# Wide value and key products in the second half of a streaming encoder step, and its queries in a new place

## The chip, the cores and the metric

One core of a Trainium2 chip. The metric is the device time of one execution of the whole kernel in microseconds, as the median of several runs, without what the host does.

## The reference

One layer of a hybrid encoder. A prompt of 2048 frames and a sample of 64 frames, both 1024 wide, go through RMSNorm and one projection to 6144 columns:

```python
h = rmsnorm(x, norm_g) @ w_in
qa, ka, va, za, qb, kb, vb, zb, ga, gb = jnp.split(h, _split_points(), axis=-1)
```

The first four parts, 512 columns each, feed differential attention with four heads: queries and keys in two halves of 64, normalised, values of 128, a linear distance term, a chunked causal mask, and the difference of two softmaxes. The next four feed retention with four heads: a recurrence over chunks of 64 frames with a state of 128 by 128 per head. `za` and `zb` gate the two branches, `ga` and `gb` (1024 columns each) merge them:

```python
m = ga * (oa @ w_oa) + gb * (ob @ w_ob)
return x + m @ w_out
```

The sample attends to 4096 cached frames as well. Normalised keys, values and the retention states are outputs too.

## The kernel before, in words

All large products take float32 operands split in two parts, high and low, of a rounded type; a product is the sum of three on TensorE: high by high, high by low, low by high. So each weight that is loaded is cast (the high part, ScalarE, line 546) and subtracted (the low part, GpSimd, line 556, or VectorE for three of the first pieces, line 553).

The prompt is projected in two halves of 1024 frames (the sample goes with the first). There are two kinds of projection. `transposed` keeps weights in the array and streams 512 frames past them; it makes retention's queries and keys and all gates. `natural` keeps a tile of 128 frames in the array and streams the columns of weights: 256 at a time ("narrow"), two tiles of frames in one bank of PSUM, or 512 at a time ("wide"), one tile in a bank. Both go through `mm_group` (line 592), eight row blocks of the input by three products each. `fin_qk`, `fin_va` and `fin_vb` normalise, split and store what comes out; keys and queries are transposed on TensorE on the way.

Attention's values, keys and queries (`va`, `ka`, `qa`) are wide in the first half and narrow in the second, in two groups of 256 columns each, that is two heads: value, key and query of heads 0 and 1, a mark `kqv0`, then those of heads 2 and 3, a mark `kqv1`. Retention's values (`vb`) follow, wide in both halves, then retention's queries and keys, a mark `ret`, and the gates. `w_stream` writes this list; `w_load` and `w_split` follow it for the weights, one piece after the other.

The projected parts go to DRAM and come back: `h_loader` loads the keys and values of a head, `q_loader` its queries, and `head_in` lets them start some time after the head's mark. `z_stream` runs attention head by head, then the sample's attention (first half), and retention; TensorE takes its products in between those of the projections. Buffers are counted by tags: four each of `K` and `V` in the attention pool, sixteen of `w` for split weights, three of `ws` for weights as loaded. Where the split weights of a wide group lie is set by its number in the list (`w_room`): groups 0 and 2 (the first half's values and queries) take the `K` and `V` buffers, the others the `w` buffers.

After the projections, `out_stream` multiplies the gated branches by their output weights (`m_tile`), then by `w_out`: `y_quad` does 256 frames at a time with seven products (`SEVEN`) in place of eight, from sums of blocks that are made ahead. `out_prep` splits the output weights and gates the rows; it starts when attention and retention are done.

What sets the order: the kernel is written by a planner in Python. Each stage is a generator; `loop` takes the first by priority whose condition or time has come, and it issues instructions until it yields. The planner holds a clock for TensorE (`self.pe`) and estimates for the other engines; a buffer taken from `take` and an operand carry the time at which they are thought to be ready. So the order on each engine is fixed before the kernel runs, by estimates, and a change to one stage moves the instructions of all that follow. All loads and stores go through the queue of SyncE.

Of the kernel before, what the change touches and what calls it, by code (L numbers as in the profile page):

```python
# [71 lines left out]
class Hybrid:  # L72
# [464 lines left out]
    def w_piece(self, wait):  # L537
# [10 lines left out]
        return self.w_low(wide, n, st, h, l, th, tag, tags)  # L548

    def w_low(self, wide, n, st, h, l, t, tag, tags):  # L550
        th = t
        if n in (5, 7, 8):
            self.nc.vector.tensor_sub(l, st, h.bitcast(F32))
            t = self.V(512, t)
        else:
            self.nc.gpsimd.tensor_sub(l, st, h.bitcast(F32))  # L556
            t = self.G(512, t)
# [157 lines left out]
    def spawn_fin(self, fin, ps, r, n, nu, t0):  # L715
        t = self.pe + LAT
        done = fin(ps[:r, :n], r, nu, t0, t) if r == 128 else self.halves(ps[:, :n], n, t, fin, t0)
        self.spawn(done, 0, "w")
# [293 lines left out]
    def q_loader(self, half):  # L1012
        for h in range(4):
            yield from self.head_in(half, h)
# [3 lines left out]
    def head_in(self, half, h):  # L1018
        k = f"kqv{h // 2}{half}"
        yield lambda: k in self.done  # L1020
        yield self.marks[k] + 9000

    def h_loader(self, half):
        for h in range(4):
            yield from self.head_in(half, h)
            yield from self.load_head(half, h)
# [898 lines left out]
    def y_quad(self, g):  # L1925
# [3 lines left out]
        for k, (bank, b, need, done) in enumerate(SEVEN):  # L1929
# [14 lines left out]
            split = (g, k) == (7, 6)  # L1944
            for ct in range(4):
# [6 lines left out]
                if split:  # L1952
                    continue
# [7 lines left out]
            if split:  # L1961
                yield lambda: "x12" in q
                for u in range(2):
                    cols = slice(256 * u, 256 * u + 256)
                    for ct in range(4):
                        csl = slice(128 * ct, 128 * ct + 128)
                        for a, w in ((h, wh), (h, wl), (l, wh)):
                            nc.tensor.matmul(ps[:, cols], a[:, csl], w[:, ct, cols], start=False,
                                             stop=w is wh and a is l and ct == 3, skip_group_check=True)
                            t = self.P(256)  # L1970
                    self.y_last(q, ps, t, cols)
                    yield self.pe
                return
# [67 lines left out]

    def y_last(self, q, ps, t, cols):
        x = self.xr[q["g"]][0]["12"]
        self.nc.vector.tensor_add(x[:, cols], ps[:, cols], x[:, cols])
        self.V(256, max(t, q["x12"]))
        t0 = 256 * q["g"]
        self.st(self.o["y_prompt"][0, t0:t0 + 128, 512 + cols.start:512 + cols.stop], x[:, cols], 1 << 17)
# [93 lines left out]
    def w_stream(self):  # L2141
# [12 lines left out]
        first = ([wva, wk, wq, m0, m1], ORD(fva0, fva, fk, fq, m0, m1))  # L2154
# [11 lines left out]
        seqs = [f + seq for f in first]  # L2166
# [6 lines left out]
        self.npiece = 0  # L2173
        self.opened = False
# [22 lines left out]
    def mark(self, name):  # L2197
        yield lambda: True
        self.done.add(name)
        self.marks[name] = self.pe  # L2200

    def z_stream(self):
        for half in range(2):
            yield lambda: f"kqv0{half}" in self.done
# [143 lines left out]
```

## Time and profile before

| what | value |
|---|---|
| median of 3 runs | 1929.06 us (1927.94 to 1929.13) |
| the profiled execution: its time | 1928.88 us |
| its span | 1927.1 us |
| granted TensorE clock | 1.0 |
| TensorE, VectorE, ScalarE, GpSimd busy | 1919.5, 1134.2, 1005.1, 461.5 us |
| moved by DMA | 308.50 MB, 160 GB/s on average |

Names: PE is TensorE, PEld its weight loads, DVE VectorE, ACT ScalarE, POOL GpSimd, SP SyncE. `L592` is line 592 of the kernel. `mm<-wh,xh` is a product into the tile `mm` with the columns of `wh` streamed past the held tile `xh`. In a row of a group, "x384 | 110.8, 289" is the count, the busy time in us and the mean of one in ns. In a row of waits stand the total in us, the times, and the longest. The busy time of a product has a modelled end, and neighbours overlap. The sample's attention lies at about 500 to 670 us of the span, the first half's retention at about 740 to 830; the second half's narrow products begin at about 740 us, the output stage at 1570, the last group of products at 1920.

### The profile page before, as it was taken

How to read it: one execution, taken by the hardware profiler on the slowest of the kernel's cores; microseconds unless marked ns; L12 is line 12 of the kernel's file. 1: busy time of each engine (PE TensorE's matmuls, PEld its weight loads, DVE VectorE, ACT ScalarE, POOL GpSimd, SP SyncE). 2: the span in 40 equal slices, each digit the busy share in tenths (PEclk: the TensorE clock that was granted, in tenths of full speed). 3: DMA queues.
4: the chain of work that ended last, by engine and by line, in shares of the span. 5: the costliest groups of instructions: out<-in, count | busy, mean ns of one | idle time of the engine just before them, and what ended most of it. 6: DMA issues, size and time to landing. Idle time of an engine off the chain costs nothing.

```text
span 1927.1 us, 32956 instructions
## 1 busy us (share of the span) xinstructions
PE 1919.5 (100%) x11638; PEld 1709.5 (89%) x11638; DVE 1134.2 (59%) x2794; ACT 1005.1 (52%) x2137; POOL 461.5 (24%) x365
## 2 busy tenths in 40 slices
PE   9999999999999999999999999999999999999999
PEld 7878899999989999999988888888889889999887
DVE  6553576635565344646856656746664339987664
ACT  6442676655445544545756756645664535554221
POOL 2320121212121223212102211121221526522442
PEclk9999999999999999999999999999999999999999
DMA  7647563436656887664334243363233758886542
GB/s 250 211 144 185 140 184 118 122 84 166 169 159 172 226 225 210 177 193 145 102 106 140 86 129 101 105 189 107 73 112 101 236 172 247 257 252 205 173 153 77
DMA packets 356343, 308.50 MB, mean 160 GB/s; under 512 B 65745, under 2 KB 313809, under 8 KB 356178
## 3 DMA queue, kind: packets, MB, share of 16 engines
q1 hardware_dynamic: 356178, 306.39, 54.4%
q8 instruction: 92, 1.51, 0.4%
q14 instruction: 73, 0.60, 0.1%
HBM read 201.38 MB, written 99.88 MB: 156 GB/s over the span
## 4 chain that ended last, share of the span: by engine, by line
PE 95%; DVE 2%; DMA 2%; ACT 0%; issue 0%; SPq 0%; DVEq 0%; ACTq 0%
PE mm L592 55%; PE s L1071 3%; PE s L1072 3%; PE at L1179 3%; PE pv L1159 2%; PE pv L1158 2%; PE pv L1157 2%; PE s L1954 1%; PE s L1956 1%; PE s L1955 1%; PE pv L1425 1%; PE pv L1538 1%; PE at L1528 1%; PE tp L794 1%; PE mm L1954 1%; PE mm L1956 1%
## 5 line engine op out<-in xcount | busy, mean ns | idle before, releaser
L592 PE MATMUL mm<-xh,wh 128*128 128x512 f32 (+2 forms) x1280 | 457.5, 357 | 0.0
L592 PE MATMUL mm<-xh,wl 128*128 128x512 f32 (+2 forms) x1280 | 452.4, 353 | 0.0
L592 PE MATMUL mm<-xl,wh 128*128 128x512 f32 (+2 forms) x1280 | 451.9, 353 | 0.0
L556 POOL TENSOR_TENSOR wl<-ws,wh 128x512 fp32r<-128x512 f32 x189 | 255.2, 1364 | 655.4 <-ACT wh L546 480.2
L592 PEld LDWEIGHTS mm<-xh,wl 128*128 128x128 f32 x1280 | 240.9, 188 | 31.2
L592 PEld LDWEIGHTS mm<-xh,wh 128*128 128x128 f32 x1280 | 241.3, 189 | 29.1
L592 PEld LDWEIGHTS mm<-xl,wh 128*128 128x128 f32 x1280 | 241.3, 189 | 28.8
L592 PE MATMUL mm<-wh,xh 128*128 128x256 f32 (+1 forms) x696 | 236.0, 339 | 0.5 <-ACT raw L759 0.3
L592 PE MATMUL mm<-wh,xl 128*128 128x256 f32 (+1 forms) x696 | 231.1, 332 | 0.1
L592 PE MATMUL mm<-wl,xh 128*128 128x256 f32 (+1 forms) x696 | 230.9, 332 | 0.0
L1194 DVE TENSOR_TENSOR atl<-at,ath 128x512 fp32r<-128x512 f32 (+1 forms) x144 | 93.0, 660 | 146.7 <-ACT ath L1192 146.7
L897 ACT COPY ev<-mm 128x512 f32<-128x512 f32 x140 | 71.4, 510 | 190.0 <-PE mm L592 155.5
L1110 ACT ACTIVATE row<-row,a_mx 128x1024 f32<-128x1024 f32 (+7 forms) x160 | 153.9, 963 | 5.0 <-DVE a_mx L1090 5.0
L1080 DVE CUSTOM_DVE_ANT_0 row<-s,dfar 128x512 f32<-128x512 f32 (+2 forms) x192 | 118.0, 631 | 58.6 <-PE s L1072 58.3
L592 PEld LDWEIGHTS mm<-wh,xh 128*128 128x128 f32 x696 | 131.9, 190 | 14.4 <-ACT raw L759 0.8
L592 PEld LDWEIGHTS mm<-wh,xl 128*128 128x128 f32 x696 | 131.9, 189 | 13.8 <-DVE xl L480 0.6
L592 PEld LDWEIGHTS mm<-wl,xh 128*128 128x128 f32 x696 | 132.0, 190 | 12.6
L546 ACT CAST wh<-ws 128x512 fp32r<-128x512 f32 x192 | 115.8, 617 | 49.9 <-PE mm L592 22.9
L1192 ACT CAST ath<-at 128x512 fp32r<-128x512 f32 (+1 forms) x144 | 78.5, 564 | 99.8 <-PE at L1179 96.9
L960 POOL TENSOR_TENSOR r_y<-r_y,r_sq 128x256 f32<-128x256 f32 x33 | 24.7, 749 | 425.6 <-DVE r_sq L957 153.8
L1071 PE MATMUL s<-K,q 128*128 128x512 f32 (+3 forms) x320 | 119.4, 377 | 0.0
L1072 PE MATMUL s<-K,q 128*128 128x512 f32 (+3 forms) x320 | 115.6, 363 | 0.0
(387 smaller groups left out, 4182.5 us busy)
## 6 DMA issues: line engine op xcount, KB each, us to landing
ws<-in_w_in_dram SPq DMA_DIRECT2D x192, 256.0 KB, 3.3
q<-qT SPq DMA_DIRECT2D x128, 128.0 KB, 3.0
V<-vN SPq DMA_DIRECT2D x24, 512.0 KB, 5.2
K<-kT SPq DMA_DIRECT2D x48, 256.0 KB, 4.3
xt<-in_x_prompt_dram SPq DMA_DIRECT2D x16, 512.0 KB, 6.0
kn<-in_cache_k_T_dram SPq DMA_DIRECT2D x32, 256.0 KB, 3.4
vc<-in_cache_v_diff_dram SPq DMA_DIRECT2D x32, 256.0 KB, 3.6
mT<-mo SPq DMA_DIRECT2D x64, 128.0 KB, 3.1
```

What stands on the lines that cost most here:

```text
L546: self.nc.scalar.copy(h, st)
L556: self.nc.gpsimd.tensor_sub(l, st, h.bitcast(F32))
L592: nc.tensor.matmul(ps, p, q, start=c == 0 and i == 0, stop=c == KC - 1 and i == 2)
L897: nc.scalar.copy(ev, ps)
L1071: nc.tensor.matmul(ps, q1s, kk, start=True, stop=False)
L1072: nc.tensor.matmul(ps, q2s, kk, start=False, stop=True)
L1080: nc.vector.tensor_tensor_reduce(out=units[k0 // 1024][:, k0 % 1024:k0 % 1024 + n], in0=ps, in1=tab, scale=-SLOPES[h], scalar=3.0e38, op0= ...
L1110: nc.scalar.activation(u, u, AF.Exp, bias=mx, scale=-1.0, accum_out=lp[:, k:k + 1])
L1157: nc.tensor.matmul(o, v0, ah[:, s0:s0 + n], start=kt == 0, stop=False)
L1179: nc.tensor.transpose(at[:, w:w + 128], src, self.ident)
L1192: nc.scalar.copy(ah[:, :w], at[:, :w])
L1194: nc.vector.tensor_sub(al[:, :w], at[:, :w], ah[:, :w].bitcast(F32))
```

## The change

Three things. In the second half attention's values and keys become wide: all four heads' values, then all four heads' keys, then a mark `kv1`. The queries stay narrow: those of heads 0 and 1 come next, with a mark `q01`; then retention's queries and keys, then retention's values, and only then the queries of heads 2 and 3, with a mark `q11`. The wide values, group 4 in the list, take the `K` and `V` buffers, and wait in the planner until the sample's four heads are done with them (`n_spv == 4`). Two pieces of weights, 114 and 116, which are those of the first two heads' queries, have their low part made on VectorE.

Second, loads of heads no longer start by time alone: `head_in` also waits until everything that was under way at the mark has been finished and its stores issued (`fins`, `finish`). Third, the last of the seven products of the last group, which was cut into two pieces of 256 columns with an addition and a store each, is done like all others.

```diff
-        elif nw in (0, 2):
+        elif nw in (0, 2, 4):
+            if nw == 4:
+                yield lambda: self.n_spv == 4
             tags, pool, shape = ("K", "V"), self.ap, [128, 2, 512]
...
-        return self.w_low(wide, n, st, h, l, th, tag, tags)
-
-    def w_low(self, wide, n, st, h, l, t, tag, tags):
+        return self.w_low(wide, n in (5, 7, 8, 114, 116), st, h, l, th, tag, tags)
+
+    def w_low(self, wide, vector, st, h, l, t, tag, tags):
...
-        if n in (5, 7, 8):
+        if vector:
...
-        if fresh and wide:
+        if fresh and wide and half == 0:
             yield from self.opening(fin)
...
+        self.spawn(self.finish(done, len(self.fins)), 0, "w")
+        self.fins.append(False)
...
+    def finish(self, done, k):
+        yield from done
+        self.fins[k] = True
...
-            yield from self.head_in(half, h)
+            yield from self.head_in(half, h, ("kqv{}0", "kv1"))
...
         yield lambda: k in self.done
+        yield lambda: all(self.fins[:self.before[k]])
         yield self.marks[k] + 9000
...
-            split = (g, k) == (7, 6)
...
-        first = ([wva, wk, wq, m0, m1], ORD(fva0, fva, fk, fq, m0, m1))
+        first = ([wva, wk, wq, m0, m1], [wva, wk, (None, "kv"), fq[0], (None, "q0")])
...
-        seqs = [f + seq for f in first]
+        seqs = [first[0] + seq, first[1] + seq[1:5] + seq[:1] + [fq[1], (None, "q1")] + seq[5:]]
```

How instructions move, at three places. On TensorE, the first products of the second half before; `xl_118` belongs to the first half's last gate, the others are values of heads 0 and 1:

```order
L592 MATMUL mm<-xl_118,wh 128x320
L592 MATMUL mm<-xh_117,wl 128x320
L592 MATMUL mm<-wh,xh_8443 128x256 [waits Activation_49]
L592 MATMUL mm<-wl,xh_8443 128x256 [waits Pool_49]
L592 MATMUL mm<-wh,xl_8444 128x256 [waits DVE_49]
L592 MATMUL mm<-wh,xh_8443 128x256
```

And after; the values of all four heads:

```order
L594 MATMUL mm<-xl_118,wh 128x320
L594 MATMUL mm<-xh_117,wl 128x320
L594 MATMUL mm<-wh,xh_8462 128x512 [waits Activation_49]
L594 MATMUL mm<-wl,xh_8462 128x512 [waits Pool_49]
L594 MATMUL mm<-wh,xl_8463 128x512 [waits DVE_49]
L594 MATMUL mm<-wh,xh_8462 128x512
```

Each product of 256 columns has become half a product of 512; the held tile is loaded once for both.

On TensorE after, the step from the wide keys (`xh_8556`, the last tile of frames) to the narrow queries of heads 0 and 1, whose weights take buffers that the keys give back:

```order
L594 MATMUL mm<-wh,xh_8556 128x512
L594 MATMUL mm<-wl,xh_8556 128x512
L594 MATMUL mm<-wh,xl_8557 128x512
L594 MATMUL mm<-wh,xh_8462 128x256 [waits DVE_49,Activation_49]
L594 MATMUL mm<-wl,xh_8462 128x256 [waits Pool_49]
L594 MATMUL mm<-wh,xl_8463 128x256
L594 MATMUL mm<-wh,xh_8462 128x256
L594 MATMUL mm<-wl,xh_8462 128x256
L594 MATMUL mm<-wh,xl_8463 128x256
L594 MATMUL mm<-wh,xh_8462 128x256 [waits Activation_49]
L594 MATMUL mm<-wl,xh_8462 128x256 [waits DVE_49]
```

A query product follows the last key product at once, and waits for ScalarE's cast and GpSimd's or VectorE's low part.

On VectorE, the last additions of the kernel; before, with the last group's fourth block `at` in two pieces:

```order
L2052 TENSOR_TENSOR xr<-mm,xr 128x512
L2044 TENSOR_TENSOR xr<-at,xr 128x256
L2052 TENSOR_TENSOR xr<-s,xr 128x512
L2044 TENSOR_TENSOR xr<-at,xr 128x256
L2344 UNCONDITIONAL_BRANCH
```

And after:

```order
L2012 TENSOR_TENSOR cap<-at,cap 128x512
L2037 TENSOR_TENSOR xr<-mm,xr 128x512
L2037 TENSOR_TENSOR xr<-s,xr 128x512
L2037 TENSOR_TENSOR xr<-at,xr 128x512
L2332 UNCONDITIONAL_BRANCH
```

The addition into `s` now stands ahead of the only one from `at`.

Two counts from the order that the prediction uses: between the last product of retention and the first of the output stage stood 342 products of projections, and there stand 246; between the sample's last value product and the first product of the second half stand 277 rows after the change. The first score product of attention in the first half comes 36 products later than before.

More of the change, by code (lines that the diff above doesn't have):

```diff
@@ L1013, in q_loader, with head_in @@
         for h in range(4):
-            yield from self.head_in(half, h)
+            yield from self.head_in(half, h, ("kqv{}0", "q{}1"))
             for p in range(4 * half, 4 * half + 4):
                 yield from self.load_q(h, p)
-    def head_in(self, half, h):
-        k = f"kqv{h // 2}{half}"
+    def head_in(self, half, h, names):
+        k = names[half].format(h // 2)
         yield lambda: k in self.done
+        yield lambda: all(self.fins[:self.before[k]])
         yield self.marks[k] + 9000
@@ L1024, in h_loader @@
         for h in range(4):
-            yield from self.head_in(half, h)
+            yield from self.head_in(half, h, ("kqv{}0", "kv1"))
             yield from self.load_head(half, h)
@@ L1960, in y_quad @@
                     yield self.pe
[L1961 to L1973, printed above, removed]
             self.give("og", t, 2)
@@ L2040, in y_p3 @@
         yield from self.y_add(q, 0, 1, ps, bank, max(t, q["x12"]))
[L2042 to L2047, printed above, removed]
     def y_add(self, q, a, n, ps, bank, t):
@@ L2173, in w_stream @@
         self.npiece = 0
+        self.n_spv = 0
+        self.fins, self.before = [], {}
         self.opened = False
@@ L2200, in mark @@
         self.marks[name] = self.pe
+        self.before[name] = len(self.fins)
     def z_stream(self):
         for half in range(2):
-            yield lambda: f"kqv0{half}" in self.done
+            yield lambda: ("kqv00", "kv1")[half] in self.done
             if half == 0:
```

3 lines of the change are left out of this document (removed).

## The prediction

> **What bounds the kernel now.** I read the page first, then who waits for whom on TensorE, then the chain of work that ended last in pieces, and last the timelines of the end and of the step from the projections to the output stage. The page's lines on the span, on TensorE and on the chain:
>
> ```profile
> span 1927.1 us, 32956 instructions
> PE 1919.5 (100%) x11638; PEld 1709.5 (89%) x11638; DVE 1134.2 (59%) x2794; ACT 1005.1 (52%) x2137; POOL 461.5 (24%) x365
> PE 95%; DVE 2%; DMA 2%; ACT 0%; issue 0%; SPq 0%; DVEq 0%; ACTq 0%
> ```
>
> TensorE is busy for 1919.5 of 1927.1 us and carries 95% of the chain. All it waits for in the whole run is this (us in total, times, longest):
>
> ```profile
> PE at L420 <- DVE epst L2272: 1.1, 1, 1.1
> PE at L1968 <- DVE xr L2044: 0.6, 1, 0.6
> PE pv L1425 <- DVE atp L1456: 0.5, 1, 0.5
> PE at L1828 <- DVE ogl L1784: 0.4, 1, 0.4
> PE mm L592 <- ACT raw L759: 0.3, 1, 0.3
> PE tp L472 <- DVE xt L458: 0.3, 1, 0.3
> PE mm L661 <- ACT wh L546: 0.3, 1, 0.3
> PE mm L592 <- DVE tlo L840: 0.2, 1, 0.2
> ```
>
> That is 3.7 us, 1.1 of it before the first product. So there is nearly no wait to win back: the time is the sum of TensorE's steps. A change gains what it takes from that sum, and loses what it adds in waits.
>
> **The price of a step.** Busy time can't be used: neighbouring products overlap in the rows. What counts is start to start, and the chain gives it, since it merges products that follow each other without a break (start, us, what, count). Narrow products (256 columns) in the second half, undisturbed and between other work; then wide ones (512 columns): two runs from the first half's keys, two from its queries, one from the second half's retention values:
>
> ```profile
> 849.60 8.64 PE mm L592 x72
> 858.67 13.56 PE mm L592 x113
> 882.05 0.71 PE mm L592 x6
> ...
> 67.52 5.47 PE mm L592 x24
> 102.82 6.85 PE mm L592 x30
> ...
> 122.28 11.90 PE mm L592 x51
> 143.24 5.60 PE mm L592 x24
> ...
> 957.51 4.11 PE mm L592 x18
> ```
>
> Narrow: 8.64/72 = 0.1200 us, 13.56/113 = 0.1200, and 0.118 in the short run. Wide: 5.47/24 = 0.2279 and 6.85/30 = 0.2283 in the keys, 11.90/51 = 0.2333 and 5.60/24 = 0.2333 in the queries, 4.11/18 = 0.2283 in the values of retention. The code has one difference between these stages: the first half's values and queries have their weights in the attention's K and V buffers, keys and retention values in the pool of weights. So the two wide prices go with the place of the weights, as far as this trace can tell.
>
> **Wide values and keys in the second half.** By-form rows say how many narrow products of this orientation there are, in three such rows:
>
> ```profile
> L592 PE MATMUL mm<-wh,xh 128*128 128x256 f32 x384 | 110.8, 289 | 0.2 <-DVE tlo L840 0.2
> ```
>
> Three times 384 is 1152 for values, keys and queries. Values and keys are two thirds, 768, and become 384 wide ones; the 384 of the queries stay narrow. Removed: 768 x 0.1200 = 92.2 us. Added: values, whose weights go to the K and V buffers, 192 x 0.2333 = 44.8; keys, in the weight pool, 192 x 0.2281 = 43.8. Gain 92.2 - 88.6 = 3.6 us, all of it on the path. Bounds: all wide products at 0.228 and narrow at 0.1200 gives 92.2 - 87.6 = 4.6; all at 0.2333 and narrow at 0.118 gives 90.6 - 89.6 = 1.0. I take 3.6, since the removed products ran mostly in long stretches like those at 0.1200. Bytes loaded, splits and evictions stay the same in number, but for two splits that go from GpSimd to VectorE.
>
> The Trainium skill, page "TensorE: Matmul & The Clock Gate", section "Wait — 56ns, not 53.3ns?", has a warm product start every N/2.4 GHz plus about 2.5 ns. By that, this edit would save 384 x 2.5 ns = 1.0 us, an estimate from that page. The trace doesn't agree with so small a floor (0.1200 us at 256 columns, 0.228 to 0.233 at 512), and the rows decide.
>
> **The last product in one piece.** The end, in order of time (start, us): the wide product before it, the first and the last of each dozen narrow ones, and VectorE's additions; then the stores of the last stretch by size:
>
> ```profile
> 1919.64 0.40 PE L1956 MATMUL s<-wt43h,ml 128*128 128x512 f32 x1
> 1919.88 0.29 PE L1968 MATMUL at<-wb22h,mh 128*128 128x256 f32 x1
> ...
> 1921.18 0.28 PE L1968 MATMUL at<-wb22h,ml 128*128 128x256 f32 x1
> 1921.57 0.42 DVE L2044 TENSOR_TENSOR xr<-at,xr 128x256 f32<-128x256 f32 x1 [3.60 <-PE at L1968]
> 1921.91 0.68 DVE L2052 TENSOR_TENSOR xr<-s,xr 128x512 f32<-128x512 f32 x1
> 1922.05 0.38 PE L1968 MATMUL at<-wb22h,mh 128*128 128x256 f32 x1 [0.59 <-DVE xr L2044]
> ...
> 1923.45 0.28 PE L1968 MATMUL at<-wb22h,ml 128*128 128x256 f32 x1
> 1923.77 0.42 DVE L2044 TENSOR_TENSOR xr<-at,xr 128x256 f32<-128x256 f32 x1 [1.17 <-PE at L1968]
> ...
> out_y_prompt_dram<-xr SPq DMA_DIRECT2D x1, 256.0 KB, 2.0
> out_y_prompt_dram<-xr SPq DMA_DIRECT2D x1, 128.0 KB, 1.9
> ```
>
> Cutting the product in two was meant to hide an addition, but the second piece waits until VectorE has read the first: both lie in one bank. From 1919.88 to the end of the last addition, 1923.77 + 0.42 = 1924.19, it takes 4.31 us. In one piece: 12 x 0.2333 = 2.80 us to the end of the last step, a tail of 0.40 - 0.23 = 0.17, the 0.04 before VectorE starts, and an addition of 0.68: 3.69 us. Gain 0.6, less 0.1 for a store of 256 instead of 128 KB (2.0 against 1.9): 0.5 us. The other addition moves ahead of it, into VectorE's idle time.
>
> **What is moved.** The last two heads' queries and retention's values go behind retention's queries and keys. No product is added by that; the question is only what stops being covered.
>
> (a) The first half's loads of keys and queries wait in the planner until the stores are issued; on TensorE the first score product stands 36 wide products (36 x 0.23 = 8 us) later. Projections fill the place. Cost 0, and up to the 0.5 of the sample's wait above if its products then meet late operands.
>
> (b) The wide values wait for the sample's fourth head, since they take the K and V buffers. Behind that wait stand all later weights: one task splits them in order. In the new order 277 products stand between the sample's last value product and the first wide one, 33 us if each took only a narrow one's 0.12; eight splits take 8 x 1.36 = 10.9 by the first row here. Cost 0.
>
> ```profile
> L556 POOL TENSOR_TENSOR wl<-ws,wh 128x512 fp32r<-128x512 f32 x189 | 255.2, 1364 | 655.4 <-ACT wh L546 480.2
> L546 ACT CAST wh<-ws 128x512 fp32r<-128x512 f32 x192 | 115.8, 617 | 49.9 <-PE mm L592 22.9
> ws<-in_w_in_dram SPq DMA_DIRECT2D x192, 256.0 KB, 3.3
> ```
>
> (c) The wide keys hold all 16 weight buffers, so the first two heads' queries get theirs only as the last key tile goes. From the release to the first query product stand 23 wide products, 23 x 0.228 = 5.2 us; cast and split take 0.62 + 1.36 = 2.0. The fourth piece has no staging buffer until the first is split: 2.0 + 3.3 + 0.6 + 1.4 = 7.3 us, and it is wanted 18 narrow products after the first, at 5.2 + 2.2 = 7.4 us, a little later with transposes between. Cost 0, with about 1 us if that load is late.
>
> (d) Attention of the second half starts and ends later, so less projection work follows it. That stretch covers the loads and splits of the output weights. Last retention product to first output product now: the chain's piece of 342 wide products, the first weight load, the last gated row of the first group, the last split, and the first output product:
>
> ```profile
> 1492.93 77.56 PE mm L592 x342
> 1497.83 1.16 SPq L147 DMA_DIRECT2D wst<-in_w_o_diff_dram  x2
> 1530.46 1.56 DVE L1784 TENSOR_TENSOR ogl<-on,ogh 128x528 fp32r<-128x528 f32 x1 [0.16 <-ACT ogh L1781]
> 1539.54 1.30 POOL L1631 TENSOR_TENSOR w_o_retl<-wst,w_o_reth 128x512 fp32r<-128x512 f32 x1
> 1570.32 0.28 PE L1827 MATMUL s<-ogh,w_o_diffh 128*128 128x264 f32 x1
> ```
>
> The preparation is done at 1540.8, 47.9 us after the last retention product; the cover is 77.6 us. In the new order 246 products stand there: 246 x 77.56/342 = 55.8 us. That leaves 8 us. Cost 0; without cover each us late is a us.
>
> **Sum.** -3.6 - 0.5 = -4.1 us. The profiled execution took 1928.88 us (span 1927.1 and 1.8 around it), 0.18 below the median of 1929.06. Against the profiled execution 1924.8; against the median 1925.0, which I forecast.
>
> **Rivals.** 0.2% is 3.9 us here, about what a measurement of this kernel can tell from no change; the line lies at 1925.2, so the forecast stands close to it.
>
> *Cheap products:* the pair of narrow products costs less than 0.240. For it: 0.118 in the short run, and half of the removed products ran between attention work. Then 1.0 + 0.5 = 1.5: 1927.6, no change. Against it: the long runs at 0.1200. The page of the Trainium skill named above gives the same 1.0. Chance 0.12.
>
> *New small waits:* the load in (c) is late, and the moved sample work in (a) meets operands not ready. The present waits after the start sum to 2.6 us; as much again leaves 1.5, and half as much 2.8: 1926.3 to 1927.6, no change. For it: a spare of 0.1 us in (c). Against it: the 11638 rows of products wait for only 2.6 us now. Chance 0.14.
>
> *The cover of the output stage is gone:* the first output products wait for weights or gated rows. It decides from 55.8 us on, and turns the gain into a loss where the preparation takes 55.8 + 4.1 = 59.9 us instead of 47.9. If loads and splits met a busier queue and took half as long again, 72 us, the wait is 16 us and the time 1941. For it: VectorE has little room to catch up in this stage (busy 49.2 and 47.9 of 50 us):
>
> ```profile
> 1600.00:1650.00 50.00, 49.96 (x408) 49.67 (x407) 49.19 (x94) 26.24 (x59) 29.75 (x26) 1.00 0.88 255
> 1650.00:1700.00 50.00, 49.56 (x407) 49.35 (x406) 47.94 (x95) 29.91 (x65) 23.60 (x20) 1.00 0.92 267
> ```
>
> Against it: the preparation starts when attention is done, not at a fixed time, and meets the same projections. Chance 0.06.
>
> *More than forecast:* wide products all at 0.228, 4.6 + 0.5, and a wait or two gone: 1923.3. Chance 0.08. That the products stay narrow has no chance: the order shows 384 fewer, and 12 fewer at the end.
>
> **How the numbers follow.** The forecast case has 0.60, from 1924.0 to 1926.0; of it 0.42 lies beyond the 0.2% line and 0.18 within. Faster 0.42 + 0.08 = 0.50; same 0.18 + 0.12 + 0.14 = 0.44; slower 0.06. The range takes in both ends of the wide price and the two rivals of no change, 1923.0 to 1927.6, and leaves out the lost cover and a little at each side.
>
> **What would show it.** In the profile after: second-half chain pieces of wide products at 0.233 us (values) and 0.228 (keys); TensorE waiting some 3 us in all; about 3.7 us from the last group's first product to the end of its addition; 56 us between the last retention product and the first output product, none waiting. A wide price above 0.236 or a TensorE wait above 1 us behind the keys or at the first output products would make the forecast wrong.

## The result, and the profile after

The changed kernel takes 1939.78 us (median of 4 runs, 1937.74 to 1941.38); the kernel before took 1928.98 us in the runs beside it. The ratio is 1.0056, with a 95% interval of 1.0044 to 1.0068: slower by 10.8 us, where 4.1 us less was forecast. The profiled execution of the changed kernel took 1941.38 us, with a span of 1939.4.

The page's lines on the span, on TensorE and on the chain of work that ended last, for the changed kernel:

```profile
span 1939.4 us, 32100 instructions
PE 1922.8 (99%) x11242; PEld 1692.5 (87%) x11242; DVE 1144.9 (59%) x2795; ACT 1002.3 (52%) x2137; POOL 464.9 (24%) x363
PE 92%; DMA 3%; DVE 3%; ACT 1%; issue 1%; SPq 0%; POOL 0%; DVEq 0%; POOLq 0%; ACTq 0%
```

There are 396 products fewer, as planned, and yet the span is 12.3 us longer. The chain shows why at once: TensorE carries 92% of it in place of 95%, and transfers and VectorE carry 6%. What TensorE waited for in the changed kernel (total, times, longest, us):

```profile
PE tp L801 <- DVE raw L786: 4.1, 1, 4.1
PE at L1836 <- DVE ogl L1792: 3.0, 4, 1.0
PE pv L1165 <- ACT ath L1200: 1.3, 1, 1.3
PE at L420 <- DVE epst L2260: 1.0, 1, 1.0
PE mm L594 <- ACT xh L479: 0.9, 1, 0.9
```

Apart from the start, three places are new: 4.1 us before transposes of query tiles (at 904 us), four waits of 0.6 to 1.0 us in the output stage, and one of 1.3 us in the first half's attention (at 354 us). They sum to 8.4 us. The rest of the loss can't be seen in a list of waits: after the waits of 4.1 and 1.3 us TensorE runs at a lower clock. The stretches around them, of the changed kernel (after the bounds come the sum and PE, PEld, DVE, ACT, POOL, each with its count; then the granted clock, the share of DMA, GB/s):

```profile
354.00:356.00 2.00, 1.01 (x6) 0.80 (x7) 1.12 (x5) 2.00 (x5) 0.00 (x0) 1.00 0.25 86
356.00:358.00 2.00, 2.00 (x12) 2.00 (x12) 1.86 (x7) 1.86 (x7) 0.00 (x0) 0.66 0.00 0
358.00:360.00 2.00, 2.00 (x9) 1.96 (x8) 0.81 (x3) 0.56 (x2) 0.73 (x1) 0.50 0.00 0
360.00:362.00 2.00, 2.00 (x10) 1.62 (x9) 1.35 (x7) 1.51 (x6) 0.00 (x0) 0.99 0.24 68
...
902.00:904.00 2.00, 0.12 (x1) 0.15 (x2) 1.71 (x1) 0.00 (x0) 2.00 (x2) 0.69 0.84 237
904.00:906.00 2.00, 2.00 (x10) 2.00 (x11) 0.00 (x0) 0.00 (x0) 0.86 (x1) 0.50 0.58 171
906.00:908.00 2.00, 2.00 (x7) 1.61 (x6) 0.01 (x1) 1.71 (x4) 0.00 (x0) 0.50 0.62 196
908.00:910.00 2.00, 2.00 (x7) 1.52 (x7) 1.81 (x3) 0.58 (x2) 1.28 (x1) 0.60 0.59 190
```

PE looks full in these rows, since a slow product is a busy one. To see the loss, take the time from the start of one product to the start of the next, and subtract what a product of its size takes undisturbed (0.229 us at 512 columns, 0.120 at 256, in proportion between, 0.109 for smaller ones). Summed by stretches of the span, in us, up to the start of the last product, for the two kernels and five experiments told below (a few tenths in a row, and more at the start, mean nothing):

| stretch | before | after | e2 | e7 | e8 | e10 | e13 |
|---|---|---|---|---|---|---|---|
| 0 to 300 | 8.6 | 9.5 | 8.6 | 8.5 | 8.9 | 9.6 | 9.2 |
| 300 to 400, first half's attention | 0.0 | 3.8 | 0.0 | 1.8 | 0.0 | 2.0 | 0.0 |
| 400 to 850 | 5.9 | 7.9 | 6.5 | 9.6 | 6.5 | 9.2 | 7.0 |
| 850 to 950, keys and queries | 0.5 | 7.5 | 2.3 | 1.1 | 4.2 | 0.6 | 0.5 |
| 950 to 1500 | 2.2 | 2.2 | 2.4 | 2.2 | 2.1 | 2.6 | 2.2 |
| 1500 to 1750, output stage | -1.8 | 1.9 | 2.7 | -2.4 | 0.0 | -0.7 | 0.3 |
| 1750 to the end | 3.4 | 2.1 | 2.3 | 3.4 | 2.0 | 1.9 | 2.0 |
| sum | 18.8 | 34.9 | 24.8 | 24.2 | 23.7 | 25.2 | 21.2 |

The changed kernel loses 16.1 us against before: 7.0 around 900 us, 3.8 around 354, 3.7 in the output stage, 2.0 between 400 and 850 (0.8 of it the wide values, which count with 0.229 here and take 0.2333), and 0.9 at the start, which differs as much between other pairs of runs; 1.3 are won at the end. The sum of the undisturbed steps fell by 4.5 us, and what stands behind the start of the last product takes 0.6 us more. So the work shrank about as forecast, and some 16 us of loss came on top.

The profiled execution is the slowest of the four. Six other kernels with the same condition on the first half's loads (e1, e5, e6, e7, e10, e15; all but e7 have the changed kernel's order of instructions until 790 us at least) were profiled too: their wait at 354 us is 0.6 to 1.2 us, and the clock behind it stays at 1.00. So the low clock at 356 us, 1.5 us of the loss, seems to belong to this execution rather than to the kernel; that the median is 1.6 us shorter fits.

What answers to the rows shown of before. The chain's pieces of the changed kernel (start, us, what, count): wide values, wide keys, and the stretch between the last retention product and the first output product:

```profile
800.66 2.80 PE mm L594 x12
856.23 6.84 PE mm L594 x30
1524.55 55.80 PE mm L594 x246
```

That is 0.2333 us for a value product, 0.2280 for a key product, and 246 products in 55.8 us: the forecast's three numbers. And the end, with the last product in one piece:

```profile
1932.54 0.39 PE L1959 MATMUL at<-wb22h,mh 128*128 128x512 f32 x1
...
1935.61 0.69 DVE L2037 TENSOR_TENSOR xr<-at,xr 128x512 f32<-128x512 f32 x1 [2.11 <-PE at L1961]
```

From 1932.54 to 1935.61 + 0.69 = 1936.30 it is 3.76 us (4.31 before, 3.69 expected). From there to the end of the span, with the larger store, it is 3.1 us (2.9 before).

How the longest wait comes about is told by the chain of the changed kernel from the last query products ahead of it to the first behind it:

```profile
895.02 0.44 PE tp L801 x4
895.45 3.61 PE mm L594 x30
...
899.09 0.70 ACT thi L811
899.81 0.75 DVE tlo L812
900.87 1.13 DVE sm_y L251
902.03 1.72 DVE raw L786
903.88 1.09 PE tp L801 x4
```

Only 36 products, 4.3 us, stand between two groups of transposes (the chain leaves TensorE after 30 of them); what the second needs is ready 8.7 us after the start of the first. The late link is ScalarE's copy `thi` at 899.09, for which there is one buffer. Its row, and rows of SP's queue:

```profile
891.26 2.40 SPq L147 DMA_DIRECT2D K<-kT  x4
893.76 0.53 SPq L152 DMA_DIRECT2D qT<-thi  x1
...
899.00 0.61 SPq L147 DMA_DIRECT2D q<-qT  x1
...
899.09 0.69 ACT L811 ACTIVATE thi<-tp,gq 128x512 fp32r<-128x512 f32 x1 [3.68 <-PE mm L594]
```

The buffer is free when its last content has been stored, and that store (893.76) was issued right behind four loads of keys for the second half's first attention head, 1 MB. It landed 5.2 us later: SP's load of the stored query, which waits for it, goes out at 899.00. (The row of `thi` names TensorE as what ended ScalarE's wait, but the transposes that the copy reads were done at 895.5.) ScalarE takes its work in order, so the normalization of the next tile stands behind the copy. The 1.3 us at 354 us has the same shape:

```profile
345.91 2.56 SPq L147 DMA_DIRECT2D q<-qT  x4
348.57 0.54 SPq L152 DMA_DIRECT2D oaT<-r_o  x1
...
353.02 0.38 ACT L934 COPY r_o<-pv 128x256 f32<-128x256 f32 x1 [3.30 <-DMA oaT<-r_o]
...
354.38 0.47 ACT L1200 CAST ath<-at 128x384 fp32r<-128x384 f32 x1
```

A store from a single buffer (`r_o`) goes out behind loads of a head and lands 4.4 us later, ScalarE waits 3.30 us for the buffer, and the cast that TensorE needs stands behind it.

### The profile page after: what moved, and what is told of

Its sections match the earlier page's. It is cut to its first block, busy times and chain, and to the rows that moved or that the text cites. A ratio compares the mean times of both kernels' runs of the same rounds, so it can differ in the third digit from the quotient of the medians.

```text
span 1939.4 us, 32100 instructions
## 1 busy us (share of the span) xinstructions
PE 1922.8 (99%) x11242; PEld 1692.5 (87%) x11242; DVE 1144.9 (59%) x2795; ACT 1002.3 (52%) x2137; POOL 464.9 (24%) x363
## 4 chain that ended last, share of the span: by engine, by line
PE 92%; DMA 3%; DVE 3%; ACT 1%; issue 1%; SPq 0%; POOL 0%; DVEq 0%; POOLq 0%; ACTq 0%
PE mm L594 53%; PE s L1079 3%; PE s L1080 3%; PE at L1187 3%; PE pv L1167 2%; PE pv L1166 2%; PE pv L1165 2%; PE s L1959 1%; PE s L1961 1%; PE s L1960 1%; PE pv L1546 1%; PE at L1536 1%; PE tp L801 1%; PE at L1959 1%; PE pv L1433 1%; PE mm L1959 1%
## 5 line engine op out<-in xcount | busy, mean ns | idle before, releaser
L594 PE MATMUL mm<-wh,xh 128*128 128x512 f32 (+1 forms) x568 | 214.8, 378 | 1.2 <-ACT xh L479 0.9
L594 PE MATMUL mm<-wh,xl 128*128 128x512 f32 (+1 forms) x568 | 209.4, 369 | 0.1
L594 PE MATMUL mm<-wl,xh 128*128 128x512 f32 (+1 forms) x568 | 209.0, 368 | 0.1
L594 PEld LDWEIGHTS mm<-wh,xl 128*128 128x128 f32 x568 | 107.3, 189 | 19.6 <-DVE xl L480 0.6
L594 PEld LDWEIGHTS mm<-wh,xh 128*128 128x128 f32 x568 | 107.4, 189 | 19.0 <-ACT xh L479 1.3
L594 PEld LDWEIGHTS mm<-wl,xh 128*128 128x128 f32 x568 | 107.5, 189 | 17.1 <-DVE wl L555 0.3
L1140 DVE SCALAR_TENSOR_TENSOR row<-row,a_w 128x1024 f32<-128x1024 f32 (+4 forms) x96 | 102.4, 1076 | 22.5 <-ACT row L1137 22.3
```

What stands on the lines that cost most here:

```text
L594: nc.tensor.matmul(ps, p, q, start=c == 0 and i == 0, stop=c == KC - 1 and i == 2)
L1140: nc.vector.scalar_tensor_tensor(out=u0, in0=u0, scalar=w[:, 0:1], in1=u1, op0=ALU.mult, op1=ALU.add)
```

## The experiments

In what follows, "the gate" is the new condition that loads of heads wait until earlier stores are issued. The theory at first was: place one (850 to 950 us), store behind head loads; place two (354 us), the new gate on the first half's loads; place three, the output stage has too little cover. The main rival: wide products or the moved queries cost more than priced.

**e1, head loads of the second half behind the first queries.**

```diff
-            yield from self.head_in(half, h, ("kqv{}0", "kv1"))
+            yield from self.head_in(half, h, ("kqv{}0", "q01"))
```

> Changed kernel, but the second half's loads of keys and values for attention wait until the first two heads' queries are projected (mark q0), not only values and keys. Main theory, place one: in the changed kernel those loads stand on SP's queue ahead of the query stores that free the single buffer thi; ScalarE waits 3.68 us for it, TensorE 4.12 us (tp <- raw) at 904 us, and its clock falls to 0.54 after. With the loads behind the queries that wait and the low clock are gone: some 6.5 us less than the changed kernel's 1939.8, 1933 (1931 to 1935), and no TensorE wait over 1 us between 850 and 950 us. Rival (the wide products themselves cost more than priced, or the queries' place does): no change, 1939 to 1941. Second rival: attention starts later and the cover of the output stage shrinks further, which gives back part, 1935 to 1938.

Measured 1947.09 us; ratio to before 1.0095 (1.0081 to 1.0109). The place is cured (0.3 us lost between 850 and 950), but attention starts and ends later: only 126 products, 28.7 us, are left between the last retention product and the first output product, and the preparation takes 50.9 us. So 15.4 us are lost in the output stage; two of its waits in e1:

```profile
PE mm L1837 <- POOL w_o_retl L1639: 3.7, 1, 3.7
PE s L1836 <- DVE ogl L1792: 2.5, 1, 2.5
```

TensorE waits for weights being split there, which it does in no other run but e3. That is the rival of a lost cover in the prediction, made real, and this edit is no cure.

**e2, the first half without the gate.**

```diff
-        yield lambda: all(self.fins[:self.before[k]])
+        if half == 1:
+            yield lambda: all(self.fins[:self.before[k]])
```

> Changed kernel, without its new gate on the first half's loads (they wait for the mark and 9 us of planner time, as before, not for the stores to be issued). Main theory, place two: the gate shifts attention of the first half by 36 wide products, and that puts a 1.3 us TensorE wait (pv <- ath) at 353 us with a clock of 0.66 behind it, 3.4 us in all. Without the gate: 1936.4 (1935 to 1938), and no such wait near 353 us. Rival (that wait is chance, or has its cause elsewhere): no change, 1939 to 1941.

Measured 1931.16 us; 1.0011 (1.0002 to 1.0020): 8.6 us less than the changed kernel, more than expected. Place two is gone (3.8 to 0.0), and place one shrinks from 7.5 to 2.3 as well. From 878 us of the changed kernel on, TensorE's products come in the same order in both, with the same 36 between those transposes, and the query's store stands behind the four loads of keys in e2 too; yet TensorE doesn't wait there (e2's wait of 1.6 us, at 877 us, is at earlier transposes). The orders of ScalarE and SP differ a little until 908 and 915. In e2 the last tile's key store (`kT<-thi`) lands 2.3 us after its issue, where it took 5.2 in the changed kernel, so the loads and the query's store behind it go out some 3 us earlier, measured by TensorE's products. The moved loads alone do not make the long wait, then; the traffic into which the gate shifts them is part of it. Of e2's waits:

```profile
PE at L1837 <- DVE ogl L1793: 2.1, 2, 1.5
PE tp L801 <- DVE raw L786: 1.6, 1, 1.6
```

So taking the gate away wins most of the loss, at two places. (The wait of 1.5 us in the output stage, at 1649 us, has a clock of 0.50 behind it; the two together cost 3.0 us.)

**e3, both edits.**

> Changed kernel with both edits: second half's head loads behind the first queries, first half's gate away. Main theory: the two places add up, 6.5 + 3.4 = 9.9 us less than the changed kernel, 1930 (1928 to 1932); what stays against before is the thinner cover of the output stage, some 3 us, less the 4 us forecast. Rival: the two act on the same thing, or something else costs the 10.8 us: 1933 or more.

Measured 1947.11 us; 1.0096 (1.0082 to 1.0110), as e1: with the cover gone, what is won earlier doesn't show. The sum of the two edits was a wrong expectation.

**e4, the kernel before with a late preparation of the output stage.**

```diff
+        yield self.pe + 22000
         self.spawn(self.out_prep(), 1)
```

> The kernel before, with the preparation of the output stage (its loads, splits and gated rows) started 22 us of planned time later, so that some 55.6 us of projections cover it in place of 77.6: the cover that the changed kernel has, with nothing else of it. Main theory, place three: fewer gated rows stand ready when the output products begin, VectorE has no room to catch up, and TensorE waits for gated rows (at <- ogl) 3 to 4 times by about 0.9 us: 3 us more than the kernel before, 1932 (1931 to 1933). Rival (the prediction's: 8 us of spare are enough): no change, 1928 to 1930.

Measured 1928.32 us; 1.0003 (0.9994 to 1.0012): no change. The last split of output weights ends at 1560.0 us, 9.2 us ahead of the first output product (10.7 in the changed kernel), and TensorE waits 1.0 us for gated rows in all. So the shorter cover costs nothing by itself, as the prediction said, and my theory on place three falls.

**e5, the first head's keys loaded by GpSimd's queue.**

```diff
+        eng = self.nc.gpsimd if (half, h) == (1, 0) else self.nc.sync
...
-                    tk = self.ld(k[o:o + 64].bitcast(F32), ..., 1 << 18)
+                    tk = self.ld(k[o:o + 64].bitcast(F32), ..., 1 << 18, eng)
```

> Changed kernel, but the keys of the second half's first head are loaded by GpSimd's queue instead of SP's; their place in the planner stays. In the changed kernel those four loads stand on SP until the keys' stores have landed (SP idle from 887.1 to 891.3 us, then 2.4 us for the four), and the query's store that frees thi stands behind them. Theory, place one, by order in the queue: without them on SP the store leaves 1.7 us earlier, ScalarE's wait of 3.68 us shrinks to 2 or less, TensorE's 4.12 us wait and the low clock after it go: some 6.4 us less than 1939.8, 1933 (1932 to 1936). Rival (the bytes collide in the 16 DMA engines, whichever queue issues them): TensorE's wait there stays 2 us or more and the time is 1937 to 1941.

Measured 1939.83 us; 1.0057 (1.0044 to 1.0069): no gain, the rival holds. From e5's timeline, the query stores on SP, which now leave at once, GpSimd's loads, and VectorE's copy that waits:

```profile
889.63 0.36 SPq L152 DMA_DIRECT2D qT<-thi  x1
890.42 0.36 SPq L152 DMA_DIRECT2D qT<-tlo  x1
893.73 6.09 SPq L147 DMA_DIRECT2D q<-qT  x4
...
890.19 1.52 POOL L147 DMA_DIRECT2D K<-kT  x3 [0.24 <-issue]
...
898.68 0.75 DVE L812 SCALAR_TENSOR_TENSOR tlo<-tp,gq,thi 128x512 fp32r<-128x512 f32 x1 [4.89 <-DMA qT<-tlo]
```

Here `thi` lands 4.1 us after its issue (SP's load that waits for it goes out at 893.73), but `tlo`, issued among the loads, lands 8.2 us after its issue, and VectorE waits in ScalarE's place. TensorE waits 4.0 us, as before. TensorE, VectorE and ScalarE have the changed kernel's order throughout. So it isn't the order in SP's queue alone, but the bytes: 1 MB of loads and the stores share the same DMA engines. (The Trainium skill says as much in "DMA: Bandwidth & Descriptors", section "Issuing engines are not separate DMA queues": transfers of all issuing engines run on the same 16 and interleave. The 8.2 us agree.)

**e6, head loads one query tile later.**

```diff
-        yield lambda: all(self.fins[:self.before[k]])
+        n = self.before[k] + (k == "kv1")
+        yield lambda: len(self.fins) >= n and all(self.fins[:n])
```

> Changed kernel; the second half's head loads wait until the stores of the first query tile are issued too, one tile later than in the changed kernel, where e1 had them some 20 us later. Theory, place one: the query's store isn't behind the loads, the 4.1 us wait at 904 us and the low clock are gone, and attention starts only a tile (6 to 8 us) later, so the output stage keeps 48 us of cover or more for a preparation of 47.9: 1933 (1931 to 1937), where e1's 1947 came from the output stage. Rival (e1's time shows that the loads were not the cause): 1939 or more.

Measured 1932.83 us; 1.0024 (1.0014 to 1.0034), 7.0 us less than the changed kernel. The loss between 850 and 950 us is 0.5 us, with half of the key loads behind the first query's stores. Up to the place of the long wait TensorE, VectorE and ScalarE have the changed kernel's order, so that wait went by the place of the loads alone. Together with e5: what matters is which bytes are ahead of the stores. The output stage keeps its 246 products of cover and still waits 3.4 us.

**e7, the kernel before with the gate alone.**

```diff
+        if half == 0:
+            yield lambda: all(self.fins[:self.before[k]])
```

> The kernel before, with the changed kernel's gate on the first half's loads alone (they wait until the stores are issued); the second half is as before. Theory, place two: the first half is then the changed kernel's, the wait pv <- ath at 353 us and its low clock cost 3.4 us: 1932.1 (1931 to 1934). The run without the gate lost 8.6 us, of which 5.2 lay near 875 to 905 us; if the gate costs those also with narrow values and keys, the time is 1937. Rival (the gate harms only together with the wide second half): 1928 to 1930.

Measured 1934.32 us; 1.0027 (1.0018 to 1.0036): 5.6 us more than before, with narrow values and keys. The gate harms without anything else of the change: 1.8 us around 354, 3.7 between 400 and 850 (1.8 of it one wait at 811 us, `tp <- raw`), 0.6 between 850 and 950. Its wait at 353 us is 1.0 us, and no low clock follows it:

```profile
352.00:354.00 2.00, 0.94 (x6) 0.48 (x4) 0.58 (x2) 1.98 (x5) 0.00 (x0) 1.00 0.24 86
354.00:356.00 2.00, 1.97 (x15) 1.97 (x15) 2.00 (x7) 1.97 (x7) 0.00 (x0) 1.00 0.15 51
```

**e8, as e2, and the queries stay where they were.**

```diff
-        seqs = [first[0] + seq, first[1] + seq[1:5] + seq[:1] + [fq[1], (None, "q1")] + seq[5:]]
+        seqs = [first[0] + seq, first[1] + [fq[1], (None, "q1")] + seq]
```

> Changed kernel without the gate on the first half (as e2, 1931.2), and with the last two heads' queries and retention's values where they stood before, ahead of retention's queries and keys; values and keys stay wide. Theory (moving queries costs nothing by itself, the loss is in waits at the places named): within 1.5 us of e2, 1930 to 1932.5. Rival (the moved queries and values cost what e2 still lacks against the forecast of 1925.0): 1925 to 1928.

Measured 1929.53 us; 1.0003 (0.9994 to 1.0012), 1.6 us less than e2. The cover is shorter here (216 products, 49.1 us), and the output stage loses less (0.0 against 2.7). VectorE, ScalarE and GpSimd do that stage in another order than in the changed kernel, whose order e2, e5 and e6 share.

**e9, e8 with the edit of e6** (in the second half alone).

> e8 (no gate on the first half, queries and retention's values where they were, 1929.5) and the edit of e6 (second half's head loads behind the first query tile's stores). It has none of the three places: no shift of the first half, loads not ahead of the first query's stores, an output stage in the order of e8. Theory: 1929.5 or up to 2 us less, 1927.5 to 1929.5, since e8's waits near 915 to 930 us (1.7 us) come from the same traffic. Rival (e6 gained by chance of order): 1930 or more.

Measured 1927.68 us; 0.9995 (0.9986 to 1.0004). e8's wait of 1.7 us between 900 and 950 us (s <- a_acc) is gone, that of 1.6 us at 875 (tp <- raw) is left.

**e10, the changed kernel with three more splits on VectorE.**

```diff
-        return self.w_low(wide, n in (5, 7, 8, 114, 116), st, h, l, th, tag, tags)
+        return self.w_low(wide, n in (5, 7, 8, 114, 116, 117, 118, 119), st, h, l, th, tag, tags)
```

> Changed kernel; three more splits of weights, those that GpSimd runs at 900.7 to 904.9 us beside the late normalization, go to VectorE (0.68 us each in place of 1.3). Theory: part of the 4.1 us wait at 904 us is VectorE slowed by GpSimd (the steps sm_t and raw take 1.1 and 1.7 us there in place of 0.17 and 0.69); without it the wait is 2 to 3 us and the low clock after it shorter or gone: 1935 to 1938.5. Rival (the store's landing alone sets the wait): 1939 to 1941.

Measured 1929.46 us; 1.0004 (0.9995 to 1.0013): 10.3 us less than the changed kernel, far more than the theory had. (The expectation named the wrong splits: the three that move run at 878.7 to 883.0 us in the changed kernel.) Between 850 and 950 us no more is lost than before the change, and the output stage stands in the order of e8 and loses nothing.

**e11, the kernel before with the last product in one piece.**

> The kernel before, with the last product in one piece and nothing else of the change. The prediction's term: 0.5 us less than before, 1928.2 (1927.7 to 1928.7). Rival (the single addition and the larger store give it back): 1928.7 to 1929.2. By the clock on the wall the two can hardly be told apart; the profile's end tells them, by the time from the last group's first product to the end of its addition: 3.7 us, or 4.3 and more.

Measured 1928.73 us; 1.0000 (0.9991 to 1.0008). The median doesn't tell 0.5 us; the end does: first product at 1919.92, the addition from 1923.00 for 0.69, so 3.77 us, and 3.1 from there to the end.

**e12, e8 with the three splits on VectorE.**

> e8 (1929.5), with three more splits on VectorE, those that GpSimd runs at 873.7 to 877.9 us. There TensorE waits 1.56 us (tp <- raw) and VectorE's steps sm_y and raw take 1.27 and 1.72 us in place of 0.17 and 0.69. Theory (GpSimd's splits slow VectorE): that wait shrinks to 0.5 us or less, 1928.5 (1927.5 to 1929.3). Rival (ScalarE's order sets it): the wait stays 1.3 us or more, 1929.5.

Measured 1928.06 us; 0.9995 (0.9986 to 1.0004). The 1.6 us wait is gone. VectorE in e8, with GpSimd's three splits beside it from 873.73 to 877.93:

```profile
873.77 1.27 DVE L251 SCALAR_TENSOR_TENSOR sm_y<-sm_t,sm_y 128x8 f32<-128x8 f32 x1
875.08 1.72 DVE L786 TENSOR_TENSOR raw<-raw,sm_y 128x512 f32<-128x512 f32 x1
```

And the same two steps in e12:

```profile
874.96 0.17 DVE L251 SCALAR_TENSOR_TENSOR sm_y<-sm_t,sm_y 128x8 f32<-128x8 f32 x1
875.16 0.69 DVE L786 TENSOR_TENSOR raw<-raw,sm_y 128x512 f32<-128x512 f32 x1
```

VectorE is faster there, but the planner, too, has set the transposes 12 products later, since it counts VectorE as busier. Two explanations were left, which e15 and e16 part.

**e13, everything that helped:** no gate in the first half, head loads behind one query tile, queries where they were, three splits on VectorE.

> All remedies together: no gate on the first half, head loads of the second half behind the first query tile's stores, queries and retention's values where they were, three more splits on VectorE. e9 (1927.7) still had the wait of 1.6 us near 875 us (tp <- raw), which the three splits took away in e12. Theory: the waits add up, so 1927.7 - 1.7 = 1926.0 (1925 to 1927): that is nearly the forecast of 1925.0, so wide values and keys and the single last product bring about what was forecast, once their side effects are gone. Rival (the remedies act on the same microseconds, or wide pieces cost more than priced): 1927.5 or more.

Measured 1925.79 us; 0.9985 (0.9976 to 0.9994): faster than both kernels, by 3.1 us than before. Of its waits the longest, the start's aside, are 0.7 us:

```profile
PE at L420 <- DVE epst L2262: 1.1, 1, 1.1
PE at L1838 <- DVE ogl L1794: 1.0, 3, 0.7
PE mm L594 <- ACT xh L479: 0.7, 1, 0.7
```

**e14, as e13, with the queries moved as in the change.**

> As e13, but the last two heads' queries and retention's values moved as in the changed kernel. e10 (1929.5: the changed kernel with the three splits on VectorE) less what the first half's gate costs (1.5 us at 353 us and some 3 us between 650 and 800): theory, moving them costs nothing by itself: 1926 (1925 to 1927.5). Rival (moving them costs a wait of its own, or brings the output stage's slower order back, 2.5 us): 1928 to 1929.5.

Measured 1929.39 us; 1.0005 (0.9996 to 1.0014): the rival, 3.6 us more than e13. The two profiles can't show what it is made of: e14's is its fastest run (1928.34), e13's its slowest (1927.51), and their spans differ by 0.9 us. e14's output stage stands in the changed kernel's order, e13's in that of e8.

**e15 and e16, the plans of e10 and e12 with the three splits back on GpSimd.**

```diff
         if vector:
-            self.nc.vector.tensor_sub(l, st, h.bitcast(F32))
+            eng = self.nc.gpsimd if self.npiece in (117, 118, 119) else self.nc.vector
+            eng.tensor_sub(l, st, h.bitcast(F32))
             t = self.V(512, t)
```

> e10 with the plan kept and the engine put back: the planner counts the three splits as VectorE's, so every other instruction stands as in e10, but GpSimd runs them, as in the changed kernel. (They are the three at 878.7 to 883.0 us of the changed kernel; the expectation of e10 took them for those at 900.7.) Theory, order: what e10 gained came from the plan, which sets transposes behind more products (69 in place of 30 ahead of the late ones) and gives the output stage another order; the time stays 1929.5 (1928.5 to 1931) and no TensorE wait over 1 us lies between 850 and 950 us. Rival, port: it came from VectorE no longer slowed by GpSimd; the wait comes back, 1933 or more.

> e12 with the plan kept and the engine put back, as e15 to e10. In e12 the transposes at 877 us stand 12 products (1.4 us) later than in e8, and VectorE's row raw ends 0.9 us earlier. Theory, order: the later transposes alone hide the chain, no wait over 0.5 us at 877 us, 1928.1 (1927.3 to 1929). Rival, port: the wait of 1.6 us comes back at least by half, 1929 to 1930. VectorE's rows sm_y and raw near 875 us tell whether GpSimd's splits slow them: 1.2 us and 1.7 us, or 0.17 and 0.69.

Measured 1929.93 us (1.0008, 0.9999 to 1.0017) and 1927.77 us (0.9997, 0.9988 to 1.0005): as e10 and e12. The traces have e10's and e12's order on TensorE, VectorE, ScalarE and GpSimd, the three splits aside; in SP's queue one pair of transfers (e16) or two (e15) change places. In e16 VectorE is slow again beside GpSimd, and no wait of TensorE follows there:

```profile
873.87 1.27 DVE L251 SCALAR_TENSOR_TENSOR sm_y<-sm_t,sm_y 128x8 f32<-128x8 f32 x1
875.17 1.74 DVE L787 TENSOR_TENSOR raw<-raw,sm_y 128x512 f32<-128x512 f32 x1
```

The chain of e15 at the place of the long wait:

```profile
890.91 0.44 PE tp L802 x4
891.35 9.91 PE mm L595 x69
901.25 0.44 PE tp L802 x4
```

69 products stand between the transposes in place of 36, 9.9 us in place of 4.3, and the late chain (8.7 us in the changed kernel) fits below them. (The expectation's 30 is the chain's piece.) So what e10 won is a matter of the plan alone; on which engine these three splits run is worth 0.5 us or less. Three other splits ran on GpSimd from 900.70 to 904.86 in the changed kernel, and VectorE's `sm_y` and `raw` beside them took 1.13 and 1.72 us. No run took those away with the order kept, so what they add to the 4.1 us wait isn't shown.

## Why the prediction was wrong, point by point

**Wide values and keys: right.** The prices of 0.2333 and 0.228 us came as read from the first half, and the undisturbed steps fell by 4.5 us at flat prices. e13, without most of the side effects, is 3.1 us faster than before, where 4.1 were forecast; of the 2.4 us that its profile loses more than before's, 2.1 are in the output stage (0.3 against -1.8). The rival of cheap products is out.

**The last product: right.** 0.55 us less to the end of the addition in the changed kernel and 0.54 in e11, where 0.6 were forecast. Of it the store gives back 0.2, where 0.1 was forecast, so 0.35 of the 0.5 are left.

**(a), the step that failed.** "Cost 0, and up to the 0.5 of the sample's wait": taking the gate off the first half's loads wins 8.6 us in the changed kernel (e2), and adding it costs 5.6 us in the kernel before (e7). I asked what fills TensorE while attention starts later, and found projections. I did not ask what else the shift moves: the loads of heads now go out together with stores from single buffers (`r_o`, `thi`), the stores land late, ScalarE or VectorE wait for the buffer, in order, and TensorE's operands stand behind that.

**The moved head loads of the second half were not priced at all.** The prediction followed the weights of the queries (c), and there nothing waits; it did not follow the loads of keys and values, which the new mark lets go just when the first query tiles are stored (4.1 us of waiting and low clock after it, 7.0 in all). The prediction's own sign of being wrong, a wait above 1 us behind the keys, came here. e6 shows that moving these loads alone removes the wait, e5 that it is the bytes and not the issuing queue, e15 that a plan with more products between the transposes hides the same lateness, and e2 that without the gate the same place passes without a wait. The two omissions act together, so their costs can't be added.

**The rival of new small waits** was the right kind with the wrong size: it was priced by the present waits, 2.6 us in all. A wait that is there now says little on one that isn't yet; the rows that would have priced it are those of stores landing beside loads. And it left out the lower clock after a wait: 2.4 us at 904 us, and 1.5 at 356 in the one execution that had it there.

**(d), the cover, half right.** 246 products, 55.8 us, no wait at the first output product, and e4 shows that the late preparation by itself costs nothing. But "Cost 0" for the output stage is wrong: it loses 3.7 us more than before. A shorter cover isn't what goes with the loss: the seven profiled runs in e8's order (e8, e9, e10, e12, e13, e15, e16), with 216 products of cover, have -0.9 to 0.3 there, and those in the changed kernel's order, with 246 (e2, e5, e6, e14), 2.7, 2.2, 1.8 and 0.0. But the order alone doesn't set it either: from 1477 us on these four have the changed kernel's order on every engine, SP too, and e14 loses nothing. What is lost are waits for gated rows (`ogl`), with a clock of 0.50 behind those of e2 and e5. What makes them long or short stays open.

**(b) and (c): right.** TensorE waits neither for wide values' weights nor for those of the queries behind the keys. With the queries moved the time was longer by 1.6 us (e2 against e8) and 3.6 us (e14 against e13); in the first pair the output stage accounts for it (2.7 against 0.0), in the second it isn't shown.

## What to carry to other kernels

Where a planner fixes the order ahead, a change of any stage is also a new draw of all that stands close behind: ask for each load that it lets go at another time which stores from a single buffer are under way then, and which engine, in order, waits for that buffer. Price such a wait by how late a store lands beside a megabyte of loads (here 4 to 8 us in place of some 2.5), not by the waits of the kernel at hand. A plan can hide lateness that can't be removed, if it sets the step that needs the operand some microseconds later; so it may pay to give a planner's estimate some reserve at those steps, which no run here tried by itself.

## What the runs showed of the hardware

A wait costs more than itself. Behind the 4.1 us wait the granted clock was 0.50 to 0.60 for some 6 us, and products of 512 columns started 0.427 us apart. The Trainium skill, "TensorE: Matmul & The Clock Gate", section "HAM oscillation — how this bites in real kernels", has idle gaps of over about 3.4 us bring this about; that wait agrees. But waits of 2.4 us (e5, at 1657 us), 1.5 us (e2, at 1649) and 1.3 us (the changed kernel, at 354) had a clock of 0.50 behind them too, while waits of 1.8 us (e7, at 811), 1.6 us (e2, at 877) and 1.2 us (e5, at 354) had none. So the measurements differ from the page here: a shorter wait may do it too, and the length alone doesn't tell.

VectorE's instructions beside GpSimd's splits took 1.27 and 1.72 us in place of 0.17 and 0.69.
